# A hybrid decoder block on one core: other product times, and a debt of small products, in the planner that orders TensorE

## The chip, the cores and the metric

The kernel runs on one core of one Trainium2 chip. The metric is the device time of one execution, in microseconds (us). The kernel before takes 3546.21 us (median of 3 runs, 3540.18 to 3557.44).

## What is computed

One layer over 2048 tokens of width 1024, all in float32. The part that matters here is the first half, a mixer made of two groups of eight heads:

```python
def retention_mixer(p, positions, gn_w, gn_b):      # eight heads, chunks of 128 tokens
    ...
    y = retention_chunkwise(q, k, v)
    return jax.nn.silu(g) * head_group_norm(y, gn_w, gn_b, GN_EPS_RET)

def rwkv7_mixer(p, mu, w0, w_up, a0, a_up, g_up, k_k, k_a, r_k, gn_w, gn_b):
    p = token_shift(p, mu)                          # eight heads, one state of 64x64 each
    ...
    y = wkv7_scan(r, decay, k, v, -kk, kk * a)      # a recurrence over all tokens
    ...

def reference(...):
    h = rmsnorm(x, norm_mix); p = h @ w_in
    x = x + concat(retention_mixer(p[:RET]), rwkv7_mixer(p[RET:])) @ w_out
    x = x + memory_cross_attention(rmsnorm(x, norm_xattn), rmsnorm(mem, norm_mem), w_q, w_kv, w_o)
    x = x + square(relu(rmsnorm(x, norm_mlp) @ w_up)) @ w_down
    return rmsnorm(x, norm_final)
```

## The kernel before

The program has two stages. Stage 1 makes both mixers and the products of the memory's weights; stage 2 makes the output projection, the cross-attention and the MLP. Only stage 1 is touched by the change. Large products are made with operands split into a high and a low part, three products for one.

Stage 1 is written as eight generators, which the function `weave` (line 257) interleaves (line 1027): `chains, diagonals, pgs, preps, heads, posts, turns, dense`. The tokens are in four blocks of 512, the eight RWKV heads in four pairs, so there are sixteen units n = 0 to 15, block n // 4 and pair n % 4.

- `dense` makes the large products, 256 or 512 columns wide: the projections `mm..k`, `mm..r`, `mm..v`, `mmwa`, `mmg`, `mmsg`, `rmv`, `rmq`, and after them, in `memory`, `pskv`, `psqk` and `psvo`. It follows `PLAN`, and takes an item only when its condition holds. Items "K" and "R" of unit n want `("P", n - 2)`: the preparation of the unit two before must be finished.
- `preps` prepares a unit (`pz, pa, pss, pm, psc, pvt, pk, pb`). In its middle it hands a triangular matrix on, through DRAM, to `diagonals`, whose 30 VectorE instructions invert 16x16 blocks (tile `Tb`), and their result goes through DRAM again into `TT`. `pgs` (`ph`, `pg`) completes the inverse in six steps.
- `chains` is the recurrence (lines 597 to 635). A unit has eight chunks, and a chunk is a step of three hops: `ch<-X,AR` on TensorE, a copy to `rh` on VectorE; `ch<-rh,TT`, then a scaling into `X` on ScalarE and on VectorE; `ch<-X,BKt`, then two instructions of VectorE into the next `X` or `Sst`. The products into `Y` stand beside them. The chain of unit n + 1 starts from the state of unit n where both share a head pair, and in any case waits for the tile `Y` of unit n.
- `heads` is retention (`prR, pqR, rsR, rYR, pvrR, pRR`), `posts` normalises and gates (`pvr, pR, pgt`), `turns` transposes the input (`psta`).

`weave` keeps a clock `now` of TensorE's work. Of the streams whose condition holds, it takes the first in the list that is due; the stream's next piece issues its products, `now` goes forward by their times, and the piece's yielded number is how long the stream then rests. Where none is due, `now` jumps. The times come from `mm` (line 140): columns over 2400 for split products, four times that for float32 ones, and fixed figures for narrow ones; `tr` has one for transposes. While `te["pin"]` is set, every product is kept in this order on TensorE (line 137). The other engines' instructions are placed by the scheduler.

Stage 2 starts with the products `o` of the output projection. Its TensorE instructions stand after stage 1's.

Of the kernel before, what the change touches and what calls it, by code (L numbers as in the profile page):

```python
# [8 lines left out]
F32 = mybir.dt.float32  # L9
# [9 lines left out]
P = 128  # L19
# [30 lines left out]
def _split_2pi(parts, bits):  # L50
    out, rest = [], TWO_PI
    for _ in range(parts):
# [6 lines left out]
    return out  # L59


PLAN = ((0, "A"), (0, "K"), (0, "R"), (1, "K"), (1, "R"), (0, "Q"), (2, "K"), (2, "R"), (0, "G"), (0, "L"),
        (3, "K"), (3, "R"), (1, "Q"), (2, "Q"), (3, "Q"))
AHEAD = 15
# [63 lines left out]
def hybrid_block(tc, a, out, dbg=None, halves=2, stages="012"):  # L128
    nc = tc.nc
    V, A, G, TE, SY, AQ = nc.vector, nc.scalar, nc.gpsimd, nc.tensor, nc.sync, nc.scalar  # L130

    te = dict(pin=False, queue=False, us=0.0)

    def pinned(ins, us):

        if te["pin"]:
            tc.keep_in_program_order(ins)
            te["us"] += us

    def mm(o, l, r, start, stop):  # L140
        n = int(np.prod(r.shape[1:])) / 2400
        us = n if r.dtype != F32 else 4 * n if n > 0.05 else 0.03 if n < 0.02 else 0.084
        pinned(TE.matmul(o, l, r, start=start, stop=stop), us)  # L143

    def tr(o, i, idn, upper=False):

        if upper:
            mm(o, i, idn, True, True)
        else:
            pinned(TE.transpose(o, i, idn), 0.107 * i.shape[0] / P)  # L150

    top = ExitStack()
    dram = top.enter_context(tc.tile_pool(name="dram", bufs=1, space=DRAM))
# [87 lines left out]
    def chain3(ps, terms):  # L241

        n = len(terms)
        for i, ((lh, ll), (rh, rl)) in enumerate(terms):
            mm(ps, lh, rh, i == 0, False)
            mm(ps, lh, rl, False, False)
            mm(ps, ll, rh, False, i == n - 1)
# [9 lines left out]
    def weave(streams):  # L257


        now = 0.0  # L260
        live = [[g, 0.0, None] for g in streams]
        while live:
            able = [s for s in live if s[2] is None or s[2]()]
            assert able, "no stream can go on"
            s = next((s for s in able if s[1] <= now), None)
            if s is None:
                now = min(s[1] for s in able)
                continue
            s[2] = None
            te["us"], te["now"] = 0.0, now  # L270
            try:
                y = next(s[0])
            except StopIteration:
                live.remove(s)
                continue
            now += te["us"]
            if callable(y):
                s[1], s[2] = now, y
            else:
                s[1] = now + y  # L280


    if "1" in stages:
        with ExitStack() as ctx:
# [30 lines left out]
            def transpose_x(b, t, xt):  # L315
                for g in range(2):
                    ps = ps_sc.tile([P, 4, P], F32, tag="sc", name=f"psta{b}{t}{g}")
                    for j in range(4):
                        k = 4 * g + j
                        tr(ps[:, j, :], xt[:, k * P : (k + 1) * P], ident)  # L320
                    ks = slice(4 * g, 4 * g + 4)
                    A.activation(out=hT[0][:, t, ks], in_=ps, func=AF.Copy)
                    V.tensor_tensor(out=hT[1][:, t, ks], in0=ps, in1=hT[0][:, t, ks].bitcast(F32), op=ALU.subtract)
                    yield 1.2
# [75 lines left out]
            def rwkv_prep(n, pr, tok0, kS, wa, nm):  # L400
# [107 lines left out]
                for g in range(2):  # L508
                    pk = ps_sc.tile([P, 4, P], F32, tag="sc", name=f"pk{nm}_{g}")
                    for i in range(4):  # L510
                        tr(pk[:, i, :], BK[:, 4 * g + i, :, :], ident)
                    for h in range(2):
                        x = gp.tile([P, 4, C], F32, tag=f"X{h}", name=f"X{h}{nm}_{g}", bufs=4)
                        A.activation(out=x[hs[1 - h]], in_=pv_[hs[1 - h], g4[g], :], func=AF.Copy)
                        X[h].append(x)
                    yield 0.8
                    bt = gp.tile([P, 4, P], F32, tag="BKt", name=f"BKt{nm}_{g}", bufs=4)
                    A.activation(out=bt, in_=pk, func=AF.Copy)
                    BKt.append(bt)
# [133 lines left out]
            def spread(st2, nm, new):  # L653

                rb = new("rb")
                A.activation(out=rb.rearrange("p (a v) -> p a v", v=64), in_=st2.unsqueeze(2).broadcast_to([P, 8, 64]), func=AF.Copy)
                yield LAT[9]
                pR = ps_rt.tile([P, BLK], F32, tag="rt", name=f"pR{nm}")
                for t in range(4):
                    tr(pR[:, t * P : t * P + P], rb[:, t * P : t * P + P], ident)  # L660
                return pR
# [231 lines left out]
            def dense():  # L893

                for b in range(nb):
# [22 lines left out]

                    plan = list(PLAN)
                    while plan:  # L920
# [104 lines left out]

            te["pin"] = True
            weave([chains(), diagonals(), pgs(), preps(), heads(), posts(), turns(), dense()])
            te["pin"] = False


    if "2" in stages:
        with ExitStack() as ctx:
# [172 lines left out]
            for hf in range(halves):  # L1205
# [62 lines left out]
                last = None  # L1268
                for c in range(2):
# [8 lines left out]
                    last = st  # L1278
# [24 lines left out]
                last = None  # L1303
                for fb in range(8):
# [16 lines left out]
                    last = st  # L1321
# [92 lines left out]
```

## Time and profile before

| | |
|---|---|
| median of 3 runs | 3546.21 us (3540.18 to 3557.44) |
| profiled execution, its own time | 3551.9 us |
| its span, first to last instruction | 3550.0 us |
| TensorE busy | 3386.1 us, 95% |
| VectorE / ScalarE / GpSimd busy | 2059.9 / 1232.9 / 1604.6 us |
| mean granted TensorE clock | 0.968 |
| stage 1, until the first `o` starts | 1596.3 us |

The page divides the span into 40 slices; a digit is the busy share of a slice in tenths, and PEclk is the TensorE clock that was granted, in tenths. A timeline row has the start, the duration, the engine, the line, the operation and its tiles; equal instructions that follow each other are one row, and "x4" counts their records. A float32 matmul leaves two records, so "x4" of `ch` are the products of the two heads of a pair. Lines are those of the kernel before; names have their buffer numbers left out.

### The profile page before, as it was taken

What the parts mean: (1) busy time and instruction counts of PE and PEld (TensorE: products, weight loads), DVE (VectorE), ACT (ScalarE), POOL (GpSimd) and SP (SyncE); (2) the same over time, 40 slices, a digit from 0 to 9 for tenths busy, and PEclk for the clock granted to TensorE, in tenths of its full rate; (3) what the DMA queues carried; (4) which work ended last, traced back from release to release, by engine and by line L of the source; (5) the groups of instructions that cost most, each with busy time, mean ns of one, the idle gap of its engine ahead of it and who ended that gap; (6) DMA issues with size and microseconds to landing.
All of it is one profiled execution on the core that took longest, in us unless ns stands there. A gap on an engine that the chain in (4) does not pass through costs nothing.

```text
span 3550.0 us, 60462 instructions
## 1 busy us (share of the span) xinstructions
PE 3386.1 (95%) x24832; PEld 2770.6 (78%) x24832; DVE 2059.9 (58%) x3589; ACT 1232.9 (35%) x2002; POOL 1604.6 (45%) x1261
## 2 busy tenths in 40 slices
PE   7899989999999999989999999999999999999998
PEld 6667776877787778778887888888778878888886
DVE  5655555455545554452766565665747665656556
ACT  4342323132323232333434333333434353333333
POOL 5454323232323232343546555455655465555555
PEclk9889998999899889999999999999999999999999
DMA  7334332333233322284111111111351111111111
GB/s 264 134 130 154 134 97 89 116 133 110 91 103 131 117 85 95 93 300 145 46 49 48 48 48 54 48 59 48 110 182 47 42 48 48 48 54 53 54 51 50
DMA packets 147172, 333.55 MB, mean 94 GB/s; under 512 B 52048, under 2 KB 62800, under 8 KB 146896
## 3 DMA queue, kind: packets, MB, share of 16 engines
q1 hardware_dynamic: 129632, 299.43, 25.5%
q10 hardware_dynamic: 17264, 30.26, 2.4%
q8 instruction: 195, 3.19, 0.4%
q14 instruction: 81, 0.66, 0.1%
HBM read 269.34 MB, written 60.29 MB: 93 GB/s over the span
## 4 chain that ended last, share of the span: by engine, by line
PE 77%; DVE 12%; issue 3%; ACT 3%; DMA 3%; POOL 3%; SPq 0%; ACTq 0%; DVEq 0%; POOLq 0%
PE up L143 20%; PE rmq L143 5%; PE o L143 4%; PE tms L143 4%; PE mmsg L143 3%; PE m3d L143 3%; PE m6d L143 3%; PE ch L143 2%; PE m4d L143 2%; PE m2d L143 2%; PE m1d L143 2%; PE m5d L143 2%; PE m7d L143 2%; PE rmv L143 2%; DVE xr L1141 2%
## 5 line engine op out<-in xcount | busy, mean ns | idle before, releaser
L143 PE MATMUL up<-uc,whi 128*128 128x512 f32 x2048 | 633.2, 390 | 5.6 <-ACT uc L1112 5.6
L143 PEld LDWEIGHTS up<-uc,whi 128*128 128x128 f32 x2048 | 384.4, 188 | 86.8 <-ACT uc L1112 6.6
L143 PE MATMUL up<-uc,wlo 128*128 128x512 f32 x1024 | 398.9, 390 | 0.0
L186 POOL TENSOR_TENSOR wlo<-wraw,whi 128x1024 fp32r<-128x1024 f32 x103 | 252.3, 2451 | 283.4 <-ACT whi L185 269.2
L185 ACT ACTIVATE whi<-wraw 128x1024 fp32r<-128x1024 f32 x175 | 184.7, 1058 | 401.7 <-PE up L143 139.9
L612 POOL TENSOR_SCALAR Sd<-X,PC 64x64 f32<-64x64 f32 x256 | 120.2, 469 | 327.0 <-DVE X L631 313.1
L186 DVE TENSOR_TENSOR wlo<-wraw,whi 128x1024 fp32r<-128x1024 f32 x72 | 103.0, 1430 | 258.9 <-ACT whi L185 255.6
L186 POOL TENSOR_TENSOR wlo<-s,whi 128x1024 fp32r<-128x1024 f32 x60 | 159.3, 2656 | 179.2 <-ACT whi L185 179.2
L143 PEld LDWEIGHTS up<-uc,wlo 128*128 128x128 f32 x1024 | 192.2, 188 | 40.1
L143 PE MATMUL tms<-whi,ub 128*128 128x256 f32 x1024 | 192.2, 286 | 0.0
L186 POOL TENSOR_TENSOR wlo<-bd,whi 128x1024 fp32r<-128x1024 f32 x64 | 165.9, 2593 | 51.8 <-ACT whi L185 51.7
L186 POOL TENSOR_TENSOR f<-au,f 128x1024 fp32r<-128x1024 f32 x40 | 112.4, 2810 | 133.0 <-ACT f L185 133.0
L143 PE MATMUL o<-whi,f 128*128 128x512 f32 x512 | 164.6, 402 | 3.9 <-issue 3.9
L143 PEld LDWEIGHTS tms<-whi,ub 128*128 128x128 f32 x1024 | 161.1, 191 | 0.4
L143 PE MATMUL rmq<-whi,hh 128*128 128x256 f32 x512 | 149.8, 292 | 0.0
L143 PE MATMUL rmq<-whi,hl 128*128 128x256 f32 x512 | 148.8, 291 | 0.0
L143 PE MATMUL rmq<-wlo,hh 128*128 128x256 f32 x512 | 148.4, 290 | 0.0
L143 PE MATMUL tms<-wlo,ub 128*128 128x256 f32 x512 | 145.4, 284 | 0.0
L1300 ACT ACTIVATE au<-up 128x512 f32<-128x512 f32 x128 | 75.1, 587 | 194.1 <-PE up L143 194.1
L620 ACT ACTIVATE X<-ch,rn 64x64 f32<-64x64 f32 x128 | 39.1, 305 | 284.2 <-PE Y L143 272.0
L1072 POOL TENSOR_TENSOR s<-bd,bd 128x1024 f32<-128x1024 f32 x48 | 122.2, 2547 | 33.2 <-DMA bd<-w_down 22.2
L185 ACT ACTIVATE whi<-bd 128x1024 fp32r<-128x1024 f32 x64 | 67.7, 1057 | 189.3 <-PE m2d L143 63.6
(1063 smaller groups left out, 9235.0 us busy)
## 6 DMA issues: line engine op xcount, KB each, us to landing
bd<-w_down SPq DMA_DIRECT2D x64, 512.0 KB
wraw<-w_up SPq DMA_DIRECT2D x64, 512.0 KB
whi<-kepthiw SPq DMA_DIRECT2D x45, 512.0 KB
wlo<-keptlow SPq DMA_DIRECT2D x45, 512.0 KB
whi<-kepthim SPq DMA_DIRECT2D x36, 512.0 KB
wlo<-keptlom SPq DMA_DIRECT2D x36, 512.0 KB
wraw<-w_out SPq DMA_DIRECT2D x32, 512.0 KB
xs<-x SPq DMA_DIRECT2D x16, 512.0 KB
```

The source lines that it names most:

```text
L143: pinned(TE.matmul(o, l, r, start=start, stop=stop), us)
L185: A.activation(out=hi, in_=x, func=AF.Copy)
L186: eng.tensor_tensor(out=lo, in0=x, in1=hi.bitcast(F32), op=ALU.subtract)
L612: G.tensor_scalar(out=Sd[hs[h], :], in0=X[h][g][hs[h], i, :], scalar1=PC[hs[h], c : c + 1], scalar2=None, op0=ALU.mult)
L620: A.activation(out=X[0][g][hs[0], i, :], in_=chp[hs[0], 64:128], func=AF.Copy, scale=rn[hs[0], c : c + 1])
L1072: eng.tensor_tensor(out=into, in0=x, in1=y, op=op)
L1141: V.tensor_tensor(out=xv, in0=xv, in1=ps, op=op)
L1300: A.activation(out=r, in_=ps, func=AF.Relu)
```

## The change

The planner gets another table of times, and `weave` a debt. The core of the diff:

```diff
+TIMES = ((512, (0.9, 0.86)), (128, (0.15, 0.155)), (64, (0.1, 0.14)), (32, (0.045, 0.045)), (16, (0.025, 0.025)), (1, (0.074, 0.24)))
+SMALL, PAID = 2.0, 1.6
...
     def mm(o, l, r, start, stop):
-        n = int(np.prod(r.shape[1:])) / 2400
-        us = n if r.dtype != F32 else 4 * n if n > 0.05 else 0.03 if n < 0.02 else 0.084
+        n = int(np.prod(r.shape[1:]))
+        us = n / 2400 + 0.013
+        if r.dtype == F32:
+            full = l.shape[0] == P
+            us = next(u[full] for m, u in TIMES if n >= m)
+            if n == P and full and l.shape[1] == P:
+                us = 0.27
         pinned(TE.matmul(o, l, r, start=start, stop=stop), us)
...
-            pinned(TE.transpose(o, i, idn), 0.107 * i.shape[0] / P)
+            pinned(TE.transpose(o, i, idn), 0.118 * i.shape[0] / P)
...
-        now = 0.0
+        now, debt, pays = 0.0, 0.0, False
         live = [[g, 0.0, None] for g in streams]
+        first, last = live[0], live[-1]
         while live:
             able = [s for s in live if s[2] is None or s[2]()]
             s = next((s for s in able if s[1] <= now), None)
+            pays = debt > SMALL or pays and debt > 0
+            if pays and s is not first and last in able and last[1] <= now:
+                s = last
...
             now += te["us"]
+            debt = max(0.0, debt - te["us"] / PAID) if s is last else debt + te["us"]
```

`first` is `chains`, `last` is `dense`. Every piece of another stream than `dense` adds its time to the debt, the chain's pieces too; a piece of `dense` takes off its time over 1.6. Once the debt is over 2.0, `dense` is taken instead of the other streams until nothing is owed. The chain is still taken when it is due. Where `dense` cannot go on, because its condition doesn't hold or because it has ended, the others go on as before, and owe.

No instruction is added to or taken from TensorE's stage 1; the order of its products changes throughout. Two places are shown.

The first is TensorE where stage 1 ends. Before, the last chain step stands among the products `psqk` of the memory, which `dense` makes last:

```order
L143 MATMUL psqk_3_17047<-hh,wlo_17013 128x256
L143 MATMUL psqk_3_17047<-hh,whi_17012 128x256
L143 MATMUL ch_7_16988<-X_33_1_15811,BKt_1_15858 64x64
L143 MATMUL ch_7_16988<-X_33_1_15813,BKt_1_15858 64x64
L143 MATMUL Y_16302<-SR_1_15584,X_33_1_15811 64x64
L143 MATMUL Y_16302<-SR_1_15584,X_33_1_15813 64x64
L143 MATMUL psqk_3_17047<-hl,whi_17012 128x256
```

In the changed kernel the last product of `dense`, a `psvo`, is followed by unit 13's last inverse step and the first hop of its chain:

```order
L152 MATMUL psvo_1_1_16388<-wlo_16364,hh 128x512
L152 MATMUL psvo_1_1_16388<-whi_16363,hl 128x512
L152 MATMUL pg_1_16397<-TA_15113,Mx_14440 32x32 x16
L152 MATMUL pss_16416<-cs,sq_15295 64x1 x16
L152 MATMUL pg_2_16436<-TT_162,TA_15113 32x32 x16
L152 MATMUL prR_16457<-rv_13509,rq_15037 128x128 x2
L152 MATMUL prR_16457<-rv_13584,rq_15093 128x128 x2
L152 MATMUL ch_0_16465<-X_31_0_14703,AR_31_0_14509 64x64
L152 MATMUL ch_0_16465<-X_31_0_14705,AR_31_0_14512 64x64
```

From there 316 rows of the order hold small products alone, with all of the chains of units 13, 14 and 15, the rest of the preparation of unit 14 and all of that of unit 15 after its large products, until stage 2's first `o`:

```order
L152 MATMUL Y_17624<-SR_1_17238,X_33_1_17319 64x64
L152 MATMUL Y_17624<-SR_1_17238,X_33_1_17321 64x64
L152 MATMUL pvr_17819<-cs,ysq_17815 128x2 x4
L159 MATMUL pR_17829<-cs,rb_17827 128x128 x4
L152 MATMUL pgt_17836<-ga_14305,gup_17810 128x512
L152 MATMUL pgt_17836<-g_14306,lw_17812 128x512
L152 MATMUL o_17873<-whi_16370,f_17879 128x512
```

So the large products have moved ahead of the last three chains.

The second place is TensorE at the retention heads of block 2, pair 3. Before, their products stand between a chain's hops and the large products `mm30k`, a few small ones at a time:

```order
L143 MATMUL mm30k<-hh,whi_12551 128x512
L143 MATMUL mm30k<-hl,whi_12551 128x512
L143 MATMUL prR_12558<-rv_11408,rq_12319 128x128 x2
L143 MATMUL prR_12558<-rv_11864,rq_12435 128x128 x2
L143 MATMUL ch_3_12532<-rh_3_12534,TT_162 64x64 x2
L143 MATMUL Y_12262<-AR_23_0_11362,X_23_0_11689 64x64
L143 MATMUL Y_12262<-AR_23_0_11365,X_23_0_11691 64x64
L150 MATMUL pqR_12571<-cs,rq_12319 128x128 x4
L143 MATMUL mm30k<-hh,wlo_12552 128x512
```

In the changed kernel the same heads stand in a run that begins behind a large product `rmq` and has no other in it for 85 rows, since `dense` waits there for `("P", n - 2)` (the heads' `prR` are the two rows behind those shown):

```order
L152 MATMUL rmq_12076<-whi_12016,hl 128x256
L152 MATMUL ph_1_12132<-TB_11804,Mx_11233 32x16 x32
L152 MATMUL pz_12168<-wa_7740,wua_12166 128x512
L152 MATMUL pa_12172<-wa_7740,wua_12166 128x512
L152 MATMUL ph_2_12176<-TT_161,TC_11805 16x16 x32
L152 MATMUL pg_0_12249<-cs,TT_161 32x32 x16
L152 MATMUL pvr_12268<-cs,ysq_12245 128x2 x4
L152 MATMUL pg_1_12278<-TA_11803,Mx_11233 32x32 x16
L152 MATMUL pg_2_12297<-TT_161,TA_11803 32x32 x16
L152 MATMUL pss_12316<-cs,sq_12232 64x1 x16
L152 MATMUL ch_0_12339<-X_22_0_11608,AR_22_0_11326 64x64
L152 MATMUL ch_0_12339<-X_22_0_11610,AR_22_0_11329 64x64
```

The small products that stood apart, with large ones between them, stand together.

## Rows read from the trace of the kernel before

**Rows 1.** The page: busy times, two lines of the 40 slices, the chain by engine.

```profile
PE 3386.1 (95%) x24832; PEld 2770.6 (78%) x24832; DVE 2059.9 (58%) x3589; ACT 1232.9 (35%) x2002; POOL 1604.6 (45%) x1261
...
PE   7899989999999999989999999999999999999998
...
PEclk9889998999899889999999999999999999999999
...
PE 77%; DVE 12%; issue 3%; ACT 3%; DMA 3%; POOL 3%; SPq 0%; ACTq 0%; DVEq 0%; POOLq 0%
```

**Rows 2.** Windows: start:end, length, busy time of each engine, granted clock, DMA share, GB/s.

```profile
0.00:100.00 100.00, 73.70 (x448) 59.94 (x449) 59.80 (x101) 40.73 (x60) 48.26 (x56) 0.97 0.75 263
131.50:1513.00 1381.50, 1307.02 (x14303) 1037.88 (x14303) 735.88 (x1904) 426.26 (x882) 443.84 (x688) 0.93 0.34 112
1513.00:1596.30 83.30, 71.60 (x467) 64.05 (x466) 47.64 (x70) 32.00 (x38) 34.17 (x15) 0.97 0.86 304
1596.30:3550.00 1953.70, 1904.64 (x9120) 1584.61 (x9120) 1195.94 (x1472) 720.74 (x999) 1061.96 (x489) 0.99 0.20 63
```

**Rows 3.** Tile ch: one VectorE copy of each chain step, 128 in all.

```profile
L610 DVE COPY rh<-ch x128: 209/224/227, 131.9 to 1506.5; 128x64 f32<-128x64 f32 x128
```

**Rows 4.** Timeline 1499.5 to 1506.7: the rows of one chain step.

```profile
1499.69 0.33 PE L143 MATMUL ch<-rh,TT 64*64 64x64 f32 x4
...
1500.36 0.31 ACT L620 ACTIVATE X<-ch,rn 64x64 f32<-64x64 f32 x1
...
1500.87 0.29 DVE L621 TENSOR_SCALAR X<-ch,rn 64x64 f32<-64x64 f32 x1
...
1502.44 0.34 PE L143 MATMUL ch<-X,BKt 128*64 128x64 f32 x4
...
1502.83 0.60 DVE L631 SCALAR_TENSOR_TENSOR X<-ch,PC,Sd 64x64 f32<-64x64 f32 x2 [1.67 <-PE ch L143]
...
1505.19 0.34 PE L143 MATMUL ch<-X,AR 128*64 128x64 f32 x4
...
1506.48 0.21 DVE L610 COPY rh<-ch 128x64 f32<-128x64 f32 x1
```

**Rows 5.** Timeline of TensorE, 1326 to 1387: unit 15's pm and its first ph.

```profile
1332.50 1.15 PE L143 MATMUL pm<-kk,BK 64*64 64x64 f32 x32
...
1379.09 1.05 PE L143 MATMUL ph<-cs,TT 32*32 32x16 f32 x64
```

**Rows 6.** Timeline of SyncE there: the matrix through DRAM, and the inverse back.

```profile
1334.41 3.64 SPq L470 DMA_DIRECT2D Lscr<-Mx  x8
...
1339.22 0.52 SPq L473 DMA_DIRECT2D Lb<-Lscr  x1
...
1364.10 0.50 SPq L542 DMA_DIRECT2D Tscr<-Tb  x1
1367.16 3.65 SPq L545 DMA_DIRECT2D TT<-Tscr  x8
```

**Rows 7.** Timeline of VectorE there: first and last of the 30 inversion instructions.

```profile
1348.91 0.28 DVE L535 TENSOR_TENSOR Tm<-Lb,Tb 128x120 f32<-128x120 f32 x1
...
1363.90 0.18 DVE L539 TENSOR_TENSOR Tb<-Tb,Tm 128x8 f32<-128x8 f32 x1
```

**Rows 8.** Windows: two runs without a large product, columns as in Rows 2.

```profile
657.90:675.80 17.90, 16.41 (x444) 13.48 (x442) 7.12 (x20) 7.71 (x19) 6.10 (x8) 1.00 0.04 10
1371.30:1389.60 18.30, 16.45 (x330) 12.74 (x329) 8.20 (x19) 5.28 (x14) 2.42 (x5) 0.72 0.08 24
```

**Rows 9.** Timeline of TensorE, 657.9 to 676, at full clock.

```profile
658.25 0.34 PE L143 MATMUL ch<-X,BKt 128*64 128x64 f32 x4
...
665.18 1.09 PE L143 MATMUL rYR<-sTR,rv 128*64 128x128 f32 x16
```

**Rows 10.** Timeline of TensorE, 1376.6 to 1387, at half clock.

```profile
1380.07 0.48 PE L143 MATMUL ch<-X,BKt 128*64 128x64 f32 x4
...
1385.16 1.91 PE L143 MATMUL rYR<-sTR,rv 128*64 128x128 f32 x16
```

## The prediction

> **What bounds the kernel now.** I read the page first. TensorE is busy for 95% of the span and makes 77% of the chain that ended last [rows 1], so what counts is what TensorE does in each stage. I then cut the span into stretches [rows 2]. Stage 2, from 1596.3 us, keeps TensorE busy 1904.6 of 1953.7 us at a clock of 0.99; the change does not order it, and I leave it as it is. Stage 1 has the losses. Between the first chain step and the last, from 131.5 to 1513, TensorE is idle for 74.5 us and the granted clock is 0.93. Since the clock has two levels, 0.93 means that 2 x 0.07 x 1381.5 = 193 us went at 1.2 GHz. Behind the last chain step there are 83.3 us in which `dense` alone makes the memory's products, with a DMA share of 0.86 and TensorE busy for 71.6.
>
> The chain of the recurrence is not the bound today: 128 steps in 1381.5 us [rows 2, 3] are 10.8 us a step, pauses included. The rows of a step say what it would take with nothing in between [rows 4]: `ch<-X,AR` 0.34, the copy 0.21, from the start of `ch<-rh,TT` to the end of the VectorE scaling 1.47 (1499.69 to 1501.16), `ch<-X,BKt` 0.34, the last VectorE pair 0.60, and five hand-overs of about 0.05 each (1502.44 + 0.34 to 1502.83): 3.2 us. Of these TensorE works for about 1.35 (five groups, each some 0.27 from start to start); for the rest it must have something else to do. Today that something is the large products, which stand between the hops to the end of the chain and beyond it. The question of this change is where those go.
>
> **The change part by part.**
>
> *The tail (A).* Every small piece owes, the chain's too, and a debt is paid at 1.6 us of `dense` for one. Over stage 1 that is more than `dense` has, and the order shows it: the last large product is now 316 rows ahead of stage 2. Behind it stand the whole chains of units 13, 14 and 15. That is 24 steps in series, and TensorE takes its products in the order shown, so no `o` can fill the gaps. How long? The way through it is a series of its own. Unit 14's `pm` comes some 8 us into it, behind one chain step. From a `pm` to the first `ph` of the inverse it took 46.6 us in the trace [rows 5], through DRAM twice: `Lb` is issued 6.7 us after `pm` began, the inversion runs for 15.2 us (1348.91 to 1364.08), and `TT` is issued 6.7 us after that [rows 6, 7]. That is 28.6; the remaining 18 are landings and waits in queues that the tail has less of. I take 30. In the new order unit 15's `pm` stands behind unit 14's `ph`, so it is 30 twice, with some 4 between; behind unit 15's first `ph` come about 4.5 steps of chain 14, other products in between, at 4 us, the change of `Y` (3), the eight steps of chain 15 alone at 3.2 (26), and the last post (6): 8 + 30 + 4 + 30 + 18 + 3 + 26 + 6 = 125 us. TensorE's own work in it, which leaves the stretch ahead, is 24 x 1.35 = 32 us for the steps and about 43 for two preparations, one pair of heads and three posts at durations such as 1.15 for a `pm` and 1.09 for half an `rYR` [rows 5, 9]: 75. A = 125 - 75 = +50. Bounds: all 24 steps bare and nothing else in the way, 24 x 3.2 + 9 - 75 = +11; two inverses at 46.6, +83; all steps at today's 10.8, 259 - 75 = +184. I take the first way, since it is made of rows, and give the last little weight, since today's 10.8 holds the large products.
>
> *Runs without large products ahead of it (B).* "K" and "R" wait for the preparation of the unit two before. When preparations are held back and `dense` pushed, `dense` runs through its item and then stands still until the preparation is done; the debt cannot be paid then, and the held small products come all at once. I counted both orders, each small product at its mean time in this trace. Before, 4 runs without a large product are longer than 8 us, 57 us of work in all. Now there are 18 besides the tail, with 307 us of work; the second place shown is the longest of them. Such a run costs nothing by itself: the one at 657.9 has TensorE busy for 16.41 of 17.9 us [rows 8], since heads and preparations stand between the hops. At its share of idle time 307 us of work bring 28 us. At the other end, with the chain's steps bare for half of that work (1.35 of 3.2 busy), 307/2 x (3.2/1.35 - 1) = 210 us. Most of the new runs hold heads or preparations, so they are near the first; the six steps of `ph` and `pg`, each a round to another engine, and the wait for `pm` make them worse than that. I take +55.
>
> *The clock (C).* At half clock a chain group takes 0.48 instead of 0.34, and `rYR` 1.91 instead of 1.09 [rows 9, 10]: 1.4 to 1.75 times. With 1.6, the 193 us at 1.2 GHz hold 193 x (1 - 1/1.6) = 72 us of loss, and no more than that can come back. The short runs, of two us with three of large products behind them, should give some back. The 18 long ones and the tail are about 490 us; the run at 1371.3 had a clock of 0.72 [rows 8], the one at 657.9 of 1.00, so between nothing and 274 us of them fall to 1.2 GHz, at a price of 0 to 100. I set C = 0, between -55 and +60. The Trainium skill ("TensorE: Matmul & The Clock Gate", Terms) prices throttled time at one half of it; by that the 193 us would hold 97, and this sum could gain 25 more at its best end. The two pairs of rows above, 1.4 and 1.75 times, do not bear out the half for small products.
>
> *The end of `dense` (D).* The 83.3 us behind the chain, where TensorE lacked 11.7, now stand beside small products that cover the wait for weights: D = -12, from -20 to 0.
>
> *The times themselves.* They have no effect but through the order. The products and their shapes stay; the other engines have the same work, later.
>
> Sum: 50 + 55 + 0 - 12 = +93. The profiled execution took 3551.9 us, so 3645; it was 5.7 above the median of the runs, so against that I predict 3639.
>
> **The rivals.**
>
> *The clock is won and the holes close (faster).* The mechanism is the payment itself: each short run of small products has large ones behind it, and the clock stays at 2.4 GHz. For it: nearly all the time at 1.2 GHz lies where small products are dense, and rows at full clock with long runs exist [rows 8]. Against it: it must hold in the runs where `dense` cannot go on. It decides if C is near -70, B at half its low end (14) and the tail near its bare time (A = +20): -70 + 14 + 20 - 12 = -48, 3498. Chance 0.11.
>
> *It cancels (no change).* A +35, B +28, C -50, D -12: +1, 3547. For it: every term is at a value that some row shows. Chance 0.08.
>
> *The tail and the runs are much slower (slower by more).* The inverses take 46.6 as today (A = +83), the runs have twice the idle time (B = +110), and the clock falls in them (C = +25): 83 + 110 + 25 - 12 = +206, 3752. For it: the run at 0.72 [rows 8], and a `ph` that waits for its inverse holds everything behind it on TensorE. Against it: the engines beside TensorE are freer there. Chance 0.19.
>
> *The payment hardly acts.* The two places of the order exclude it.
>
> **How the numbers follow.** The forecast has 0.62, and its own range is 3590 to 3700. About 0.5%, 18 us, is what a measurement of this kernel can tell from no change. Faster by more than that: 0.11 and a little of the tail of the forecast, 0.12. Within it: 0.08. Slower: 0.80. The range that leaves out 2 in 10 reaches into the faster case and to the slower one: 3530 to 3755.
>
> **What would show it.** Right: a stretch at the end of stage 1 of 90 to 160 us with only `ch`, `Y` and preparations on TensorE, busy for well under 80%, with steps of 3 to 6 us; the first `o` between 1640 and 1740; stage 2 within 10 us of its 1953.7. B: the clock and TensorE's idle time in the runs behind `rmq`. C: the mean clock from the first step to the last `psvo`, above 0.95 if the payment works. D: the stretch of `psqk` and `psvo` without the 0.86. The prediction fails if the tail is under 90 us, or if the clock ahead of it rises to 0.98 with TensorE as busy as now.

## The result and the profile after

The changed kernel takes 3711.3 us (median of 4 runs, 3709.33 to 3712.53) against 3545.39 of the kernel before beside it: 1.0462 times as long, with a 95% interval from 1.0435 to 1.0489. The forecast was 3639, so the side is right and the size is not: 166 us were lost, and 93 were predicted.

The page of the changed kernel, the same four lines as [rows 1] and the span:

```profile
span 3710.2 us, 60467 instructions
...
PE 3449.7 (93%) x24832; PEld 2833.8 (76%) x24832; DVE 2059.1 (55%) x3589; ACT 1235.5 (33%) x2002; POOL 1596.6 (43%) x1261
...
PE   7998999899989899975999999999999999999998
...
PEclk9988989798898898965999999999999999999999
...
PE 76%; DVE 12%; ACT 3%; issue 3%; POOL 2%; DMA 2%; SPq 1%; ACTq 0%; DVEq 0%; POOLq 0%
```

TensorE is busy 64 us longer with the same products, and the slices show two places: in 9 of the first 16 slices the clock is below 9 tenths (6 before), and in the 18th and 19th (some 1577 to 1762 us) the busy share falls to 7 and 5 tenths and the clock to 6 and 5. The stretches that answer to [rows 2], cut at the first chain step, the last large product and the first `o`:

```profile
0.00:127.70 127.70, 103.36 (x954) 85.07 (x954) 79.19 (x140) 53.60 (x85) 64.77 (x69) 0.99 0.69 236
127.70:1578.60 1450.90, 1328.21 (x13246) 1081.99 (x13247) 705.63 (x1749) 418.09 (x822) 424.77 (x636) 0.90 0.35 118
1578.60:1754.90 176.30, 110.93 (x1520) 80.85 (x1520) 73.38 (x227) 40.26 (x93) 43.01 (x66) 0.60 0.16 55
1754.90:3710.20 1955.30, 1907.20 (x9120) 1585.91 (x9120) 1200.89 (x1475) 723.50 (x1002) 1064.01 (x490) 0.99 0.20 63
```

Stage 2 takes 1955.3 us, and took 1953.7: nearly the whole difference is in stage 1, which takes 1754.9 for 1596.3. The last large product ends at 1578.6, and behind it stand the 176.3 us of the tail, with TensorE busy for 63% of them at a clock of 0.60. Ahead of it the clock is 0.90, where it was 0.93.

Split into TensorE's idle and busy time up to the first `o`, the 158.6 us are 97.6 of idle time (114.8 before, 212.4 now) and 61.0 of busy time (1481.5 before, 1542.5 now) with no product added. The latter is the clock: by the trace's clock records stage 1 has 433 us at 1.2 GHz, where it had 192, and the same products took no longer at 2.4 GHz than before.

**The tail, step by step.** Its first and its last rows of TensorE that carry the series of the forecast, unit 14's `pm`, its first `ph`, unit 15's `pm` and `ph`, chain 15's first hop and the last hop, and the first `o`:

```profile
1578.51 0.69 PE L152 MATMUL pg<-TA,Mx 32*32 32x32 f32 x32
...
1585.88 1.15 PE L152 MATMUL pm<-kk,BK 64*64 64x64 f32 x32
...
1620.76 0.30 PE L152 MATMUL ph<-cs,TT 32*32 32x16 f32 x6
...
1626.68 2.18 PE L152 MATMUL pm<-kk,BK 64*64 64x64 f32 x32
...
1669.22 1.05 PE L152 MATMUL ph<-cs,TT 32*32 32x16 f32 x64
...
1695.50 0.48 PE L152 MATMUL ch<-X,AR 128*64 128x64 f32 x4 [0.37 <-DVE Sst L646]
...
1728.88 0.48 PE L152 MATMUL Y<-SR,X 64*64 64x64 f32 x4
...
1736.56 1.42 PE L152 MATMUL pgt<-g,lw 96*128 96x512 f32 x1
1754.94 0.80 PE L152 MATMUL o<-whi,f 128*128 128x512 f32 x1 [16.96 <-ACT f L194]
```

From here each leg can be read: 7.3 us to the first `pm` (8 forecast), 34.9 to `ph` (30), 5.9 to the next `pm` (4), 42.5 to its `ph` (30), 26.3 to the start of chain 15 (21), 33.9 for its eight steps (26), 8.6 for the post (6), and 17.0 from the end of `pgt` to the first `o`, for which nothing was forecast. So the series was the right one, and every leg of it but the first was longer.

The largest single shortfall is the 17.0, a wait that the forecast did not have. ScalarE's rows at the seam:

```profile
1738.90 0.33 ACTq L703 DMA_DIRECT2D yscr<-yo  x1
1745.95 1.43 ACTq L1238 DMA_DIRECT2D ay<-yscr  x3
1747.42 1.06 ACT L194 ACTIVATE whi<-wraw 128x1024 fp32r<-128x1024 f32 x1 [12.75 <-issue]
...
1753.83 1.06 ACT L194 ACTIVATE f<-ay 128x1024 fp32r<-128x1024 f32 x1 [5.35 <-DMA ay<-yscr]
```

The loads of stage 2's first blocks `ay` are issued at 1745.95, 7 us behind the last write of stage 1, and `o` waits for `f`, which waits for that load. Before, the memory's large products covered this way: the last `yscr` was written at 1532.5 and the first `f` made at 1543.7, and those products ran on to 1592.4. Now they end 176 us ahead of `o`. In the kernel before the first `o` starts 3.9 us after the last of them (1592.4 to 1596.3).

The second of the `pm` to `ph` legs, 42.5 us, is not the inverse alone. Rows of SyncE, ScalarE and TensorE ahead of that `ph`:

```profile
1656.14 4.35 SPq L560 DMA_DIRECT2D TT<-Tscr  x8
...
1663.00 0.31 ACT L684 ACTIVATE lw<-gup 96x128 fp32r<-96x128 f32 x1 [5.37 <-DMA gup<-lora]
...
1664.93 1.11 PE L159 MATMUL pk<-cs,BK 128*128 128x128 f32 x4 [4.48 <-ACT X L529]
```

The loads of `TT` had landed by 1662.3 (semaphore records of the trace), 35.6 us after `pm`. But TensorE's order has `pk` and some other products ahead of `ph`; `pk` waited 4.48 us for ScalarE, which had itself stood 5.37 us for the load `gup` of a post. These last 6.9 us of the leg are a wait in the order.

The last five steps of chain 15, alone on TensorE, are 3.8 us apart. One of them:

```profile
1710.80 0.48 PE L152 MATMUL ch<-X,AR 128*64 128x64 f32 x4 [0.38 <-DVE X L646]
1711.60 0.48 PE L152 MATMUL ch<-rh,TT 64*64 64x64 f32 x4 [0.32 <-DVE rh L625]
...
1713.31 0.48 PE L152 MATMUL ch<-X,BKt 128*64 128x64 f32 x4 [0.83 <-DVE X L636]
...
1714.59 0.48 PE L152 MATMUL ch<-X,AR 128*64 128x64 f32 x4 [0.38 <-DVE X L646]
```

At 0.48 a hop's group is at half clock throughout; at 0.34 [rows 4] the sum of the forecast was 3.2.

### The profile page after: what moved, and what is told of

Read it like the earlier page. It is cut to its first block, busy times and chain, and to the rows that moved or that the text cites. A ratio compares the mean times of both kernels' runs of the same rounds, so it can differ in the third digit from the quotient of the medians.

```text
span 3710.2 us, 60467 instructions
## 1 busy us (share of the span) xinstructions
PE 3449.7 (93%) x24832; PEld 2833.8 (76%) x24832; DVE 2059.1 (55%) x3589; ACT 1235.5 (33%) x2002; POOL 1596.6 (43%) x1261
## 4 chain that ended last, share of the span: by engine, by line
PE 76%; DVE 12%; ACT 3%; issue 3%; POOL 2%; DMA 2%; SPq 1%; ACTq 0%; DVEq 0%; POOLq 0%
PE up L152 19%; PE rmq L152 5%; PE o L152 4%; PE tms L152 3%; PE ch L152 3%; PE m3d L152 2%; PE m6d L152 2%; PE rmv L152 2%; PE mmsg L152 2%; PE m1d L152 2%; PE m5d L152 2%; PE m4d L152 2%; PE m7d L152 2%; PE m2d L152 2%; PE Y L152 2%
## 5 line engine op out<-in xcount | busy, mean ns | idle before, releaser
L195 POOL TENSOR_TENSOR wlo<-s,whi 128x1024 fp32r<-128x1024 f32 x60 | 159.3, 2656 | 179.1 <-ACT whi L194 179.1
```

The source lines that it names most:

```text
L195: eng.tensor_tensor(out=lo, in0=x, in1=hi.bitcast(F32), op=ALU.subtract)
```

## The experiments

All are made from the changed kernel. A table first, read from each run's profile: the time when the first `o` starts, which is the length of stage 1, TensorE's busy and idle time up to it, and the granted clock up to it. Medians stand against the kernel before on the same chip.

| run | time, us | ratio (95% interval) | first `o` | busy | idle | clock |
|---|---|---|---|---|---|---|
| before | | | 1596.3 | 1481.5 | 114.8 | 0.94 |
| changed | 3711.3 | 1.0462 (1.0435 to 1.0489) | 1754.9 | 1542.5 | 212.4 | 0.88 |
| new times, no payment | 3548.0 | 0.9992 (0.9974 to 1.0009) | 1590.4 | 1479.6 | 110.8 | 0.95 |
| payment, old times | 3699.4 | 1.0431 (1.0396 to 1.0466) | 1734.7 | 1528.7 | 206.0 | 0.88 |
| chain owes nothing | 3550.3 | 1.0005 (0.9990 to 1.0021) | 1590.3 | 1475.1 | 115.2 | 0.95 |
| no payment in memory | 3670.5 | 1.0336 (1.0314 to 1.0358) | 1718.8 | 1539.7 | 179.1 | 0.89 |
| PAID 1.4 | 3667.7 | 1.0341 (1.0315 to 1.0368) | 1713.7 | 1518.3 | 195.4 | 0.90 |
| PAID 1.2 | 3547.7 | 0.9994 (0.9969 to 1.0018) | 1586.8 | 1465.7 | 121.1 | 0.95 |
| PAID 1.0 | 3506.6 | 0.9888 (0.9868 to 0.9908) | 1549.8 | 1453.8 | 96.0 | 0.97 |
| PAID 0.8 | 3507.4 | 0.9885 (0.9860 to 0.9909) | 1556.8 | 1455.9 | 100.9 | 0.96 |
| PAID 0.8, SMALL 1.0 | 3514.3 | 0.9918 (0.9890 to 0.9947) | 1564.6 | 1458.0 | 106.5 | 0.96 |
| PAID 1.0, old times | 3531.0 | 0.9961 (0.9939 to 0.9983) | 1577.3 | 1469.5 | 107.8 | 0.95 |
| filler in the tail | 3723.4 | 1.0498 (1.0467 to 1.0529) | 1763.9 | 1576.9 | 187.0 | 0.89 |

**Which half of the change.** First the new times without the payment:

```diff
-            if pays and s is not first and last in able and last[1] <= now:
-                s = last
```

> The new product times without the debt: the payment's branch is left out. In the order the large products again end behind the last chain (no tail), and 4 runs of small products are longer than 8 us (47 us of work), none longer than 12. Theory (the debt makes the loss, the times alone do not): stage 1 as before, 1596 us within 20, time 3530 to 3570, clock about 0.97. Rival (the new times spoil the order by themselves): over 3600 us.

No change that can be measured, 1590.4 for stage 1. Then the payment with the times of the kernel before (`mm` and `tr` as they were):

> The debt and its payment with the product times of the kernel before. The order has a tail of 70 us of work and 18 more runs over 8 us (296 us of work). Theory (the debt is the cause, with any times): 3690 to 3740 us, tail near 176 us, half clock in stage 1 near 430 us. Rival (new times and debt together make the loss): under 3620 us.

3699.4, with a tail of 168.2 us. The payment makes the loss, with either table; the new times alone change nothing that can be measured.

**Is it the price?** By the planner's own times the pieces of `dense` are worth 781 of its units and all the others together 564, 159 of these the chain's. A debt of 564 at 1.6 costs 902, more than there is; it could be paid up to a price of about 1.39 (781/564), at most, since large products that are made while nothing is owed pay for nothing. The first test takes the chain's part out of the debt, which then costs 405 x 1.6 = 648:

```diff
-            debt = max(0.0, debt - te["us"] / PAID) if s is last else debt + te["us"]
+            debt = max(0.0, debt - te["us"] / PAID) if s is last else debt if s is first else debt + te["us"]
```

> As the changed kernel, but the chain's pieces add nothing to the debt. The order has no tail and 4 runs over 8 us (52 us of work). Theory (the loss is that the debt is larger than the large products can pay, since the chain owes too): tail of 176 us gone, runs gone, 3500 to 3560 us, and time at half clock under 190 us in stage 1. Rival (holding small products back is itself harmful, since preparations come late): 3600 to 3680 us, with the idle time of TensorE before the last large product still above 110 us.

3550.3: the tail is gone and the large products end last again (1588.5, the chain at 1512.1). The loss goes with the debt that cannot be paid. There is no gain, though, and four long runs remain in the order. The price was varied directly:

```diff
-SMALL, PAID = 2.0, 1.6
+SMALL, PAID = 2.0, 0.8
```

> As the changed kernel with PAID 0.8 for 1.6: a debt costs half as much. The order has no tail and no run over 8 us. Theory (the price was too high for the large products there are; paid in full it holds the clock): faster than before, 3480 to 3535 us, half clock in stage 1 under 120 us against 192. Rival (payment does not move the clock): 3540 to 3570 us with half clock about 190 us.

3507.4, faster than both kernels. Half the price, and the payment does what it was to do: between the first and the last chain step the clock is 0.96, against 0.93 [rows 2], and stage 1 has 116 us at 1.2 GHz for 192.

```profile
127.60:1459.80 1332.20, 1267.92 (x14209) 1003.22 (x14208) 730.05 (x1892) 422.97 (x870) 443.10 (x685) 0.96 0.34 115
1459.80:1556.80 97.00, 85.04 (x570) 76.77 (x569) 52.53 (x83) 38.60 (x49) 40.23 (x18) 0.98 0.80 287
```

The stretch ahead of the last chain step takes 1332.2 us for 1381.5, with TensorE busy 39 us less, 13 of them because more large products are left for the end (85.0 us busy there for 71.6). At 1.0, 1.4 and 1.2:

> As the changed kernel with PAID 1.0. All small products of stage 1 at this price are less than the large ones, so the debt can be paid; the order has no tail and no run over 8 us. Theory: as PAID 0.8, 3495 to 3525 us, half clock in stage 1 near 116 us. Rival (0.8 was a lucky order): 3535 to 3570 us.

> As the changed kernel with PAID 1.4, where the debt of all small products is about what the large ones can pay. The order has 16 runs over 8 us (275 us of work), the last a tail of 37 us of work. Theory (the loss comes with unpaid runs and with the tail, and both grow from this point on): between the two, 3600 to 3690 us. Rival (the loss is in the tail alone, and is bare chain time): under 3590 us.

> As the changed kernel with PAID 1.2. The order has no tail, but 4 runs over 8 us (60 us of work). Theory (the loss sets in where the debt outgrows the large products, between 1.2 and 1.4): near the kernel before or a little faster, 3510 to 3560 us. Rival (any price over 1.0 loses): over 3580 us.

The times are 3506.6 at 1.0, 3547.7 at 1.2, 3667.7 at 1.4 and 3711.3 at 1.6. So 0.8 was no lucky order, and the loss sets in where the arithmetic puts it, between 1.2 and 1.4. At 1.2 four runs over 8 us have come back, and with them the gain is gone. At 1.4 both parts of the loss are there, and they grow further to 1.6:

```profile
125.90:1609.20 1483.30, 1359.89 (x14050) 1099.25 (x14049) 752.23 (x1864) 442.87 (x873) 446.93 (x669) 0.92 0.34 116
1609.20:1713.70 104.50, 55.16 (x721) 39.09 (x720) 33.52 (x112) 17.77 (x42) 21.14 (x34) 0.60 0.23 84
```

**Smaller portions, and the old times at a good price.**

> SMALL 1.0 and PAID 0.8: paid in smaller portions. The order has no run over 6 us. Theory (the clock is held by short runs; shorter ones hold it no better, since small runs of 2 us already did): 3495 to 3525 us. Rival (the shorter the better): under 3495 us, half clock in stage 1 under 80 us.

> Debt with PAID 1.0 and the product times of the kernel before. The order has no tail and one run over 8 us. Theory (the gain is the affordable debt's, the new times add little): 3500 to 3535 us. Rival (the debt holds the clock only where it counts with times as measured): 3540 us or more.

Portions of 1.0 are no better than those of 2.0 (3514.3 against 3507.4). With the old times PAID 1.0 gains 0.4%, with the new ones 1.1%. So the theory's range holds, but the new times have a part in the gain. The price is hardly the reason: by the old times the small products come to 480 and the large ones to 719, so that 1.0 can be paid there too (and 1.6 cannot, about 768). What in the times makes the difference was not tested.

**Is the tail a loss of its own?** The payment was switched off from the first product of the memory on:

```diff
-            pays = debt > SMALL or pays and debt > 0
+            pays = (debt > SMALL or pays and debt > 0) and not te.get("memory")
...
+                    te["memory"] = True
                     yield from memory()
```

> As the changed kernel, but no payment once the memory's products begin. The order keeps the 18 long runs ahead of that point (307 us of work) and the large products end close to the last chain. Theory (tail and runs are separate losses; the tail holds 101 us above its work of 75, the rest about 57): the tail's loss goes, 3605 to 3650 us. Rival (the chain is late in any case and its end sets stage 1): over 3680 us. Rival (the tail is the whole loss): 3550 us.

3670.5, and both theory and rivals miss it: 41 us come back, not 101. The stretches:

```profile
129.50:1679.20 1549.70, 1420.04 (x14672) 1147.40 (x14673) 779.49 (x1956) 453.25 (x906) 465.98 (x693) 0.90 0.33 112
1679.20:1718.80 39.60, 12.85 (x91) 8.44 (x91) 6.34 (x19) 5.16 (x9) 7.90 (x9) 0.53 0.46 176
```

The large products now end at 1679.2 and the last chain at 1692.5. Of the tail 39.6 us are left: the end of the chain, then 26.3 us of post and seam, at a clock of 0.50. But the last chain ends 181 us later than in the kernel before (1511.9). It was late before the memory's first product, which starts at 1467.8 in the kernel before, at 1477.2 in the changed one and at 1479.9 in this run. The copies `rh` up to that time, one a step, in this order:

```profile
L610 DVE COPY rh<-ch x123: 209/224/227, 131.9 to 1458.8; 128x64 f32<-128x64 f32 x123
L625 DVE COPY rh<-ch x104: 204/224/227, 129.8 to 1450.1; 128x64 f32<-128x64 f32 x104
L625 DVE COPY rh<-ch x105: 172/225/227, 131.6 to 1479.3; 128x64 f32<-128x64 f32 x105
```

Of 128 steps 123 were done before, 104 in the changed kernel and 105 here. In the changed kernel none follows while the memory's products are made, since the payment takes them ahead of unit 13's last inverse step:

```profile
1477.20:1578.60 101.40, 96.83 (x677) 90.23 (x679) 49.78 (x83) 38.91 (x52) 36.97 (x17) 0.98 0.66 223
```

Here the chain goes on between them, but 23 steps are still to be made. The count goes with the long runs: it is 125 at PAID 1.0, 116 at 1.2 and 104 at 1.4. What the unpaid runs had done by then is not mended by keeping large products back for the end. The tail is where the lateness of the chains shows; the lateness comes from the runs ahead. This corrects the forecast's picture of two separate terms.

**What the clock costs in the tail.** Idle products were put into the tail, 1, 3 and 2 behind the hops of each step of units 13 to 15:

```diff
+                    if n >= 13:
+                        filler(1, f"{nm}_{c}0")
                     yield HOP[0]
...
+            def filler(k, nm):
+                ps = ps_mm.tile([P, BLK], F32, tag="mm", name=f"fil{nm}")
+                for i in range(k):
+                    tc.keep_in_program_order(TE.matmul(ps, hT[0][:, 0, 0, :], hT[0][:, :, 0, :], start=True, stop=True))
```

Their result is read by nobody, and the computation is as it was.

> The changed kernel with idle products in the tail: behind the hops of each step of units 13 to 15 stand 1, 3 and 2 products of 512 columns into a spare tile, 144 in all, whose result nobody reads; they fit into TensorE's idle time at full clock. Theory (a third of the tail's excess over the forecast is the clock at 1.2 GHz): the clock stays at 2.4 GHz, a step of chain 15 takes 3.1 to 3.4 us for 3.8, and the tail 145 to 165 us for 176. Rival (the step is bound by the other engines' hand-overs, the clock is no part of it): step 3.8 and more, tail 176 to 190.

The price of a step was settled, the remedy failed: the tail took 191.9 us, more than theory and rival gave it. In the last steps of chain 15 the clock is at 2.4 GHz, and a step takes 3.31 us with six idle products in it:

```profile
1719.09 0.34 PE L152 MATMUL ch<-X,AR 128*64 128x64 f32 x4
...
1722.40 0.34 PE L152 MATMUL ch<-X,AR 128*64 128x64 f32 x4
...
1725.71 0.34 PE L152 MATMUL ch<-X,AR 128*64 128x64 f32 x4
```

Without them, at 1.2 GHz, it was 3.79: the half clock costs about 0.5 us a step. TensorE has no idle time in these steps, so 3.31 is no less than what a step needs at full clock, and the forecast's 3.2 agrees with it. The tail as a whole grew, since the idle products added 45 us of busy time (155.9 for 110.9) and the clock, 0.71 in the mean for 0.60, did not stay up:

```profile
1680.00:1700.00 20.00, 20.00 (x126) 11.67 (x125) 3.85 (x15) 2.43 (x7) 3.96 (x9) 0.50 0.01 2
1700.00:1730.00 30.00, 30.00 (x178) 18.38 (x178) 8.42 (x29) 3.97 (x10) 7.79 (x13) 0.71 0.04 14
1719.10:1738.00 18.90, 18.90 (x151) 11.20 (x150) 6.61 (x24) 2.16 (x7) 4.85 (x11) 1.00 0.05 19
```

Between 1680 and 1700 TensorE was busy for all of the 20.0 us, and the granted clock was 0.50 throughout. There the idle products took twice their time and made steps of 5.5 us. By the clock records it rose at 1717.2, behind the post of unit 14 (`pR` and `pgt`), and from 1719.1 on the same pattern of chain groups and idle products ran at 2.4 GHz to the end of the chain.

## Why the prediction was right in its side and short in its size

**The whole.** 3711.3 us lies 11 us outside the forecast's own range (3590 to 3700), and inside the wide one (3530 to 3755) only because that one reached to the slower rival. Stage 1 lost 158.6 us, and the three parts below, 101 + 32 + 25, add up to it; +93 was forecast.

**What bounds.** Right: stage 2 moved by 1.6 us, and the loss is in what TensorE does in stage 1, where the recurrence became the bound once the large products had gone.

**A, the tail, +50 forecast, +101 measured** (176.3 less the 75 us of work by the prices of before). This is the term that was mis-sized most. The series was right. Of the 51 us that were missing, 17.0 are the seam, a wait that takes the place of the hidden one: I followed TensorE's order to the first `o`, and did not ask what `o` itself waits for when stage 1 no longer covers it. 17.4 are the two legs from `pm` to `ph`: I took 30 us for each, from bare legs, and they took 34.9 and 42.5. 10.5 of it are the inverses, which took 34.9 and 35.6, and 6.9 the wait in TensorE's order behind `pk`. 7.9 are chain 15, at half clock, and the small legs make the rest. Where a bound from rows (46.6) stands beside a sum of bare legs (28.6), the value should have lain between them and not at the low end.

**B, the runs, +55, and D, -12.** Together +43 forecast; TensorE's idle time ahead of the tail is 147.0 us against 114.8 in the whole of stage 1 before: +32. That this came near was luck. In the trace 19 stretches ahead of the tail have no large product and over 8 us of work at the mean times of before, 318 us in all. They take 487 us, and TensorE is idle for 99 of them; the four such stretches of before had 6 us of idle time. So the runs brought +93 where I took +55, by the mechanism that I gave, and the idle time outside them fell from 109 to 48 us, where I had D's 12 alone. The run shown in the order, from 1176.3 to 1218.6, and another long one:

```profile
1176.30:1218.60 42.30, 33.21 (x507) 27.32 (x506) 29.06 (x73) 15.86 (x35) 14.69 (x19) 0.72 0.19 64
1061.40:1099.60 38.20, 29.84 (x451) 23.76 (x449) 27.45 (x56) 18.88 (x39) 12.09 (x16) 0.78 0.31 99
```

TensorE is idle for 21% and 22% of them, and for 20% of all 19; 55 us for 307 us of work would have been 15%. What I missed is that the runs also make the chains late: 104 steps were done where 123 had been (above). With the payment during the memory's products this is why there are three chains in the tail.

**C, the clock, 0 forecast, +25 ahead of the tail.** TensorE is busy there for 1431.6 us, against 1481.5 less the tail's 75; in the tail the clock is a part of A. Wrong by its centre: the payment did not hold the clock, which fell to 0.90 ahead of the tail and to 0.60 in it. In the two runs above it was 0.72 and 0.78, like the run at 1371.3 [rows 8] and not like that at 657.9. What the clock costs can now be read from two runs with the same products: stage 1 has 102 us at 1.2 GHz with PAID 1.0 and 433 in the changed kernel, and busy time differs by 88.7, so a microsecond at 1.2 GHz cost 0.27 of busy time. But TensorE is idle in a part of that time: it was busy for 97 of the 102 us and for 335 of the 433 (trace and clock records). For each busy microsecond it is 88.7 in 237, 0.37, which is the 0.375 that I took from pairs of rows; the size of C failed by how long the clock was low, and not by its price. The Trainium skill ("TensorE: Matmul & The Clock Gate", Terms) prices throttled time at a half. Neither 0.27 nor 0.37 bears that out for these runs of small products.

**The rivals.** The faster one had the right mechanism for another price: with PAID 1.0 the clock is 0.97, and the kernel gains 1.1%. It failed here at the point that was named for it, the runs in which `dense` cannot go on. The slower one (3752) came nearer to the result than the forecast, 41 us off for 72. Its clock (+25) is what happened, and its tail (+83) and its runs (+110) came nearer to 101 and 93 than the forecast's +50 and +55, though the inverses took 35 us and not its 46.6; it missed that TensorE's idle time outside the runs fell. The payment that hardly acts is excluded by PAID 0.8 to 1.6.

**The signs to look for.** Of those that were named, the busy share of the tail (63%) and stage 2's time held, and so did D's: the memory's products have a DMA share of 0.66 for 0.86, with TensorE idle for 4.6 of 101.4 us. The tail's length (176 for 90 to 160), the first `o` (1754.9 for 1640 to 1740) and the clock ahead of the tail (0.90 for 0.95) did not. The steps were 3.8 us at the end, within the 3 to 6, but up to 12.5 earlier in the tail.

## A version that beats both

`SMALL, PAID = 2.0, 1.0`, all else as in the changed kernel: 3506.6 us (3504.31 to 3507.54), 0.9888 times the kernel before (0.9868 to 0.9908). Its stretches, cut at the first and the last chain step and the first `o`:

```profile
126.00:1447.40 1321.40, 1263.87 (x14182) 998.50 (x14181) 727.32 (x1895) 419.86 (x869) 433.92 (x683) 0.97 0.35 116
1447.40:1549.80 102.40, 87.04 (x594) 78.63 (x594) 53.80 (x85) 39.58 (x49) 44.22 (x21) 0.98 0.75 268
1549.80:3502.50 1952.70, 1905.26 (x9120) 1584.84 (x9120) 1196.75 (x1472) 720.80 (x999) 1062.06 (x489) 0.99 0.20 63
```

The chains end at 1447.4 us for 1511.9, and behind them 102.4 us of large products are left, which cover the seam. Of the 46.5 us that stage 1 is shorter, 27.7 are busy time and 18.8 idle time of TensorE.

## What to carry to other kernels

Before a scheduler makes one kind of work pay for another, add both up: where the price times the debtor's total is more than the payer has, the payer is used up, and what was held back comes late and alone. Then look at what the covering work covered at the seam too, since a wait that costs nothing while it is covered comes out with its full length. A price of 0.8 or 1.0, below that limit, kept the clock up here and gained 1.1%; 1.2, also below it, gained nothing.

## What the runs showed of the hardware

With chain groups and 512-column products (idle products in the tail) TensorE was busy for 20.0 of 20.0 us, and its clock stayed at 1.2 GHz for all of that time. It rose behind a post, and then the same pattern ran at 2.4 GHz for 18.9 us. A full engine in the busy column did not mean full clock. Between runs of the same products, one microsecond at 1.2 GHz cost 0.27 us of busy time, and one in which TensorE was busy 0.37, over a mixture of products that are 1.4 to 1.75 times as long there.
